# Three nine-column reciprocal roots: eleven VectorE operations each, or one GpSimd power each

## The chip, the core and the metric

One core of a Trainium2 chip runs the whole program in one launch. The metric is the device time of one execution in microseconds (us). Durations and starts come from one profiled execution; the engines are TensorE (PE in the rows, its weight loads PEld), VectorE (DVE), ScalarE (ACT), GpSimd (POOL) and SyncE (SP).

## The reference

One layer of a streaming encoder for 1024 new tokens (prompt) and 32 tokens of a running stream (sample), model width 1024. The input is normalised and projected; one half of the mixing width goes through a complex diagonal state-space scan with a gated linear unit, the other through latent attention with eight heads; each half is normalised, gated and projected back. Cut to what the change touches:

```python
def rmsnorm(x, g):
    xf = x.astype(jnp.float32)
    y = xf * lax.rsqrt(jnp.mean(xf * xf, axis=-1, keepdims=True) + EPS)
    return (y * g.astype(jnp.float32)).astype(x.dtype)

def mixer_layer(x, pos, h0, past_ckv, past_krope, p):
    h = rmsnorm(x, p['norm_in'])
    z = h @ p['w_in']
    u, g_ssm, c_q, c_kv, k_rope_raw, g_mla = jnp.split(z, cuts, axis=-1)
...
    mix = jnp.concatenate([rmsnorm(y_ssm, p['out_norm_ssm']) * jax.nn.silu(g_ssm),
                           rmsnorm(attn, p['out_norm_mla']) * jax.nn.silu(g_mla)], axis=-1)
    return x + mix @ p['w_out'], ckv, krope, h_last
```

The three norms here, of the token and of the two output halves, each need one reciprocal root per token: 1056 tokens, held as 128 partitions x 9 columns (eight columns of prompt tokens, one of sample tokens).

## The kernel before, in words

Products are done in two parts: each float32 operand is split into a rounded part and a rest (helpers `split`, `hilo`, lines 106 to 118: ScalarE rounds, VectorE subtracts), and three matmuls per product are accumulated in PSUM.

First stage (lines 206 to 304). The eight k slices of the transposed input are loaded and split. The input projection to the feature-major tiles (`mtile_mm`, line 231) takes 128 output features at a time: 8 k slices x 3 products x 3 column ranges of the 1056 tokens (384, 384, 288), 72 matmuls on line 235. Tiles 0 and 1 are accumulated while the input arrives and are copied raw to SBUF by ScalarE (line 298). The token norm is not applied to the input, but to the result: ScalarE squares the rows of x with a running sum (line 283), VectorE makes mean plus epsilon (line 284), `rsqrt` makes the root `rst` of nine columns (line 286), and `row_bcast` (line 178) turns it with nine TensorE transposes (line 185) and three ScalarE copies (line 187) into `rb`, a row of 1056 values on all partitions. `mtile_evac` (line 243) multiplies a tile with `rb` (lines 247, 251, 254). The four u tiles go through `uT`, which has two buffers, to DRAM (`u_out`, line 292) and are loaded back in another order (`load_u`). Tiles 2 and 3 are evacuated straight from PSUM, where six accumulators are set aside for these tiles, three a tile. Behind them on TensorE stand the preparations of the state-space matrices (`ssm_in`, lines 460 to 489) and the remaining eight tiles, the gates (line 720), which fill TensorE while VectorE does the scan.

Later stages: the scan (line 503), latent projections (`tok_mm`, line 572), the state-space outputs (line 677), the gated linear unit (line 705), expansion of queries and keys (lines 751 and 783, with roots of 12, 16 and 32 columns), then a half output projection (`half`, line 855) for the state-space half beside the start of the attention, the attention blocks (lines 970 to 1056), and the other half output projection at the end.

`col_rstd` (line 163) makes the root of an output half: nine matmuls with one output column sum the squares over partitions (line 170), VectorE adds epsilon (lines 172, 173), and `rsqrt` makes nine roots (line 175). For the state-space half it is `rsy` (line 728), used as a scale by ScalarE when it evacuates the products (`out_ssm`, line 885); for the attention half it is `rsa` (line 1174), called inside `half` at line 876 after the matmuls of the first two token tiles, and used by VectorE when it evacuates the products (`out_y`, line 1184). There GpSimd has added x and the other half's part before (line 1181).

`rsqrt` (line 151) is a first guess from the bits of the number (lines 155, 156) and three Newton steps of three operations (lines 158 to 160), eleven dependent VectorE operations; its two scratch buffers are a ring shared with the other roots.

What sets the order: the program is traced once, and a planner of the framework simulates it with its own costs and writes out each engine's queue: among instructions that are ready in that simulation the one that stands earlier in the program goes first. On the chip every engine works its queue strictly in that order. `issue_after` adds an edge that keeps an instruction behind another in a queue. GpSimd's queue holds, in program order, the constants at the start, the rotary tables (lines 736 to 739), the rotary products of the queries (lines 819 to 821), and, per attention block, the broadcast of the softmax sums (line 1042) and the squares, gates and splits of the output (lines 1070 to 1083), and at the end the sums of line 1181.

Of the kernel before, what the change touches and what calls it, by code (L numbers as in the profile page):

```python
# [16 lines left out]
ALU = mybir.AluOpType  # L17
# [18 lines left out]
TS = 9  # L36
# [14 lines left out]
def step(ctx: ExitStack, tc, xT, xr, winF, winT, wuq, wukv, wglu, wout, ckvcT, krcT, pk, rot, ssb, ssc, mtab,  # L51
         y_o, ckv_o, kr_o, st_o, dbg=None):
    nc = tc.nc
    pe, act, dve, pool, sp = nc.tensor, nc.scalar, nc.vector, nc.gpsimd, nc.sync
# [9 lines left out]
    def T(tag, shape, bufs=1, dt=F32, name=None):  # L64

        n = math.prod(shape[1:])
        t = sb.tile([128, -(-n // 264) * 264 if n > 400 else n], dt, tag=tag, name=name or tag, bufs=bufs)
        t = t[:shape[0], :n]
        if len(shape) == 3:
            t = t.rearrange("p (a b) -> p a b", a=shape[1])  # L70
        elif len(shape) == 4:
            t = t.rearrange("p (a b c) -> p a b c", a=shape[1], b=shape[2])
        return t

    marks = {}
# [10 lines left out]
    def PA(name="pa", tag="a"):  # L86
        return psA.tile([128, 512], F32, tag=tag, name=name, bufs=CAP[tag])
# [36 lines left out]
    def CC(n, p=128):  # L124
        taken[0] += n
        return base[:p, taken[0] - n:taken[0]]
# [12 lines left out]
    def SM(tag, shape, dt=F32, bufs=2):  # L139

        n = math.prod(shape)
        if tag not in ring:
            ring[tag] = [CC(n) for _ in range(bufs)]
        ring[tag].append(ring[tag].pop(0))
        t = ring[tag][-1].bitcast(dt)
        return t.rearrange("p (a b) -> p a b", a=shape[0]) if len(shape) == 2 else t

    onesD = CC(2)
    dve.memset(onesD[:, 0:1], 1.0 / D)
    dve.memset(onesD[:, 1:2], 1.0 / 512)  # L150
    def rsqrt(y, ms, n, p=128):

        t = SM("rq", [64])[:p, :n]
        s = SM("rqi", [64], I32)[:p, :n]
        dve.tensor_scalar(s, ms.bitcast(I32), 1, None, op0=ALU.logical_shift_right)
        dve.tensor_scalar(y.bitcast(I32), s, -1.0, float(0x5f3759df), op0=MUL, op1=ADD)
        for _ in range(3):
            dve.tensor_tensor(t, y, y, op=MUL)
            dve.scalar_tensor_tensor(t, ms, -0.5, t, op0=MUL, op1=MUL)
            r = dve.scalar_tensor_tensor(y, t, 1.5, y, op0=ADD, op1=MUL)  # L160
        return r.ins

    def col_rstd(ss, which, name):

        p = PA(name + "_p")
        ms = CC(TS)
        dve.memset(ms, 1.0)
        for i in range(TS):
            w = min(128, ss.shape[1] - i * 128)
            pe.matmul(p[:w, i:i + 1], ss[:, i * 128:i * 128 + w], onesD[:, which:which + 1],  # L170
                      start=True, stop=True)
        dve.tensor_scalar(ms[:, :TS - 1], p[:, :TS - 1], EPS, None, op0=ADD)
        dve.tensor_scalar(ms[:w, TS - 1:], p[:w, TS - 1:TS], EPS, None, op0=ADD)
        r = CC(TS)
        marks[name] = rsqrt(r, ms, TS)
        return r

    def row_bcast(r, dst):

        for c in range(3):  # L180
            p = PA("rb_p")
            n = 0
            for i in range(4 * c, min(TS, 4 * c + 4)):
                w = 128 if i < 8 else NS
                pe.transpose(p[:, n:n + w], r[:w, i:i + 1].to_broadcast([w, 128]), ident[:w, :w])
                n += w
            act.activation(dst[:, c * 512:c * 512 + n], p[:, :n], AF.Copy)
# [22 lines left out]
    for k in range(8):  # L210
# [8 lines left out]
        r = T("xr", [128, NT], 8)  # L219
# [55 lines left out]
    ssx = CC(TS)  # L275
# [7 lines left out]
        act.activation(t, t, AF.Square, accum_out=ssx[:, i:i + 1])  # L283
    dve.tensor_scalar(ssx, ssx, 1.0 / D, EPS, op0=MUL, op1=ADD)
    rst = CC(TS)
    marks["rst"] = rsqrt(rst, ssx, TS)
    row_bcast(rst, rb)
    for k in range(8):
        for j in range(2):
# [302 lines left out]
    def tok_group(gi, acc):  # L592
# [17 lines left out]
        dve.tensor_tensor(ss[:w, :n], ss[:w, :n], invn[:w, :n], op=MUL)  # L610
        dve.tensor_scalar(ss[:w, :n], ss[:w, :n], EPS, None, op0=ADD)
        rsqrt(rs[:w, :n].rearrange("p a b -> p (a b)"), ss[:w, :n].rearrange("p a b -> p (a b)"), 3 * n, w)
        kt = sm.tile([128, 4, 32], F32, tag="krt", name="krt")
        kr = sm.tile([128, 4, 32], F32, tag="kro", name="kro")
# [110 lines left out]
    for m in range(4):  # L725
        sp.dma_start(dgm[m], gate(8 + m, T("gm", [128, NT], 2), False))
    spread_s(ssy)
    rsy = col_rstd(ssy, 1, "rsy")
    mix = T("mix", [128, 4, NT])
    for m in range(4):  # L730
# [441 lines left out]
    def rsa():  # L1172
        spread_s(ssa)
        return col_rstd(ssa, 1, "rsa")
# [157 lines left out]
```

## Time and profile before

| what | us |
|---|---|
| median of three runs (583.57 to 587.38) | 585.41 |
| the profiled execution | 584.77 |
| its span, first to last instruction | 583.0 |
| TensorE busy (94%) | 547.1 |
| VectorE busy (71%), 1000 instructions | 414.8 |
| ScalarE busy (52%) | 304.4 |
| GpSimd busy (18%), 165 instructions | 107.5 |

Busy shares are means over stages with different limits. Times are from the start of the span. A timeline row gives start, duration, engine, line, operation, output and input by the program's names, shapes, how many were merged, and in brackets the engine's idle time before it and what ended that.

### The profile page before, as it was taken

The numbers are of one execution on the slowest core, as the hardware profiler recorded it, in microseconds if no ns is written. First come the engines' busy times: TensorE is split into PE (matmuls) and PEld (weight loads), VectorE is DVE, ScalarE is ACT, GpSimd is POOL, SyncE is SP. The second block draws the span as 40 slices with busy tenths as digits, with TensorE's granted clock in tenths as the row PEclk, the third lists the DMA queues.
The fourth block names the chain that finished last, engine by engine and source line by source line (L and its number), as shares of the span: only waits on it lengthen the run. The fifth ranks groups of instructions, "written<-read, shape, count | busy, mean of one in ns | idle before, by whom it ended". The sixth has DMA issues, their size and how long they took to land.

```text
span 583.0 us, 9939 instructions
## 1 busy us (share of the span) xinstructions
PE 547.1 (94%) x3707; PEld 481.5 (83%) x3707; DVE 414.8 (71%) x1000; ACT 304.4 (52%) x673; POOL 107.5 (18%) x165
## 2 busy tenths in 40 slices
PE   5989699999999997599999799999999999999997
PEld 5989599899999996599788578877778888877885
DVE  6999722989999254129989986668798577683722
ACT  5571155218135247639855966776676775752000
POOL 0000000000000010000024520222244334468330
PEclk9999799999999998889999899999999999999799
DMA  8991752232433204632401121200100101095352
GB/s 286 405 304 41 199 136 92 49 143 89 130 97 103 66 18 154 201 100 90 141 17 61 43 91 74 92 2 1 38 20 2 38 3 38 7 373 200 104 230 108
DMA packets 35266, 63.92 MB, mean 110 GB/s; under 512 B 5361, under 2 KB 21521, under 8 KB 35217
## 3 DMA queue, kind: packets, MB, share of 16 engines
q1 hardware_dynamic: 31008, 49.06, 25.9%
q10 hardware_dynamic: 4208, 14.22, 6.9%
q8 instruction: 29, 0.48, 0.3%
q14 instruction: 21, 0.16, 0.1%
HBM read 47.06 MB, written 16.21 MB: 109 GB/s over the span
## 4 chain that ended last, share of the span: by engine, by line
PE 74%; DVE 10%; ACT 5%; DMA 5%; issue 2%; POOL 2%; SPq 1%; ACTq 0%; DVEq 0%; POOLq 0%
PE mt L235 24%; PE wo L873 11%; PE ob L1048 6%; PE pt_p L1020 5%; PE S L980 3%; PE S L981 3%; PE S L982 3%; PE tk_p L585 2%; PE tk_p L584 2%; PE tk_p L586 2%; PE gl L705 2%; DMA yg<-dy 1%; PE ob L1049 1%; PE v_p L482 1%; PE qt_p L965 1%
## 5 line engine op out<-in xcount | busy, mean ns | idle before, releaser
L235 PE MATMUL mt<-xh,wh 128*128 128x384 f32 (+1 forms) x288 | 68.5, 335 | 11.9 <-ACT xh L112 6.2
L235 PE MATMUL mt<-xl,wh 128*128 128x384 f32 (+1 forms) x288 | 68.3, 331 | 0.1
L235 PE MATMUL mt<-xh,wl 128*128 128x384 f32 (+1 forms) x288 | 67.3, 330 | 0.0
L235 PEld LDWEIGHTS mt<-xh,wh 128*128 128x128 f32 x288 | 49.8, 193 | 13.5 <-ACT xh L112 6.8
L235 PEld LDWEIGHTS mt<-xl,wh 128*128 128x128 f32 x288 | 49.8, 193 | 1.0 <-issue 0.6
L235 PEld LDWEIGHTS mt<-xh,wl 128*128 128x128 f32 x288 | 49.2, 191 | 0.2 <-issue 0.2
L1020 PE MATMUL pt_p<-base,P 128*128 128x128 f32 x288 | 43.0, 276 | 0.8 <-ACT kv L769 0.7
L1048 PE MATMUL ob<-PT,kv 128*64 128x128 f32 x576 | 41.9, 279 | 0.9 <-DVE PT L1024 0.9
L873 PE MATMUL wo<-woh,mm 128*128 128x512 f32 x128 | 42.0, 398 | 0.3 <-DVE mm L110 0.3
L1048 PEld LDWEIGHTS ob<-PT,kv 128*64 128x64 f32 x576 | 32.0, 136 | 10.3 <-issue 7.2
L736 POOL TENSOR_TENSOR base<-base 128x288 f32<-128x288 f32 x1 | 0.9, 867 | 214.2 <-DVE kro L632 214.2
L1002 DVE TENSOR_REDUCE base<-S 128x1 f32<-128x1024 f32 (+3 forms) x32 | 32.4, 1017 | 10.3 <-PE S L982 10.2
L1004 ACT ACTIVATE P<-S,base 128x1024 f32<-128x1024 f32 (+3 forms) x32 | 30.6, 955 | 15.0 <-DVE base L1002 14.9
L1020 PEld LDWEIGHTS pt_p<-base,P 128*128 128x128 f32 x288 | 33.0, 140 | 5.1 <-ACT kv L769 1.0
L980 PE MATMUL S<-kTh,qTh 104*128 104x512 f32 (+3 forms) x96 | 36.2, 377 | 0.0
L1024 DVE COPY PT<-pt_p 128x512 f32<-128x512 f32 (+2 forms) x44 | 27.9, 635 | 9.3 <-PE pt_p L1020 9.1
L982 PE MATMUL S<-kTh,qTh 96*128 96x512 f32 (+3 forms) x96 | 34.2, 360 | 0.0
L981 PE MATMUL S<-kTl,qTh 96*128 96x512 f32 (+3 forms) x96 | 33.4, 348 | 0.0
L873 PEld LDWEIGHTS wo<-woh,mm 128*128 128x128 f32 x128 | 24.0, 189 | 6.2 <-DVE mm L110 0.7
L109 ACT ACTIVATE wh<-wr 128x512 fp32r<-128x512 f32 x24 | 14.1, 631 | 27.5 <-PE mt L235 25.9
L1184 DVE SCALAR_TENSOR_TENSOR yp<-wo,base,xt 128x512 f32<-128x512 f32 x16 | 11.6, 749 | 21.2 <-PE wo L873 21.2
L819 POOL TENSOR_TENSOR qx<-q,base 128x256 f32<-128x256 f32 (+1 forms) x12 | 8.3, 714 | 98.5 <-ACT q L801 83.0
(346 smaller groups left out, 1443.8 us busy)
## 6 DMA issues: line engine op xcount, KB each, us to landing
wr<-winF SPq DMA_DIRECT2D x10, 512.0 KB, 4.2
U<-du SPq DMA_DIRECT2D x8, 528.0 KB, 4.4
xr<-xr SPq DMA_DIRECT2D x8, 512.0 KB, 7.5
wor<-wout ACTq DMA_DIRECT2D x8, 512.0 KB, 4.3
dyp<-yp SPq DMA_DIRECT2D x8, 512.0 KB, 2.7
part<-dyp ACTq DMA_DIRECT2D x8, 512.0 KB, 5.3
xt<-xr ACTq DMA_DIRECT2D x8, 512.0 KB, 7.2
xr<-xT SPq DMA_DIRECT2D x7, 528.0 KB, 8.1
```

Source lines behind the costliest of these rows:

```text
L109: act.activation(hi, src, AF.Copy)
L235: pe.matmul(ps[c][:, :b - a], ww[:, k, :], xx[k][:, a:b], start=(k == 0 and first), stop=(k == 7 and last))
L584: pe.matmul(p, xhi[k][:, o:o + 128], h, start=(k == 0), stop=False)
L873: pe.matmul(s[i][c], mm[i][a][k], ww[k][b][:, c * 512:(c + 1) * 512], start=(k == 0 and first), stop=(k == 3 and last))
L980: pe.matmul(s[:, :n], qh[:, qj], kh[:, j, :n], start=True, stop=False)
L981: pe.matmul(s[:, :n], qh[:96, qj], kl[:, j, :n], start=False, stop=False)
L982: pe.matmul(s[:, :n], ql[:, qj], kh[:96, j, :n], start=False, stop=True)
L1002: dve.tensor_reduce(rl[:, 2 + j:3 + j], sf, AX.X, ALU.max, negate=True)
L1004: marks["exp", u] = act.activation(t[:, :n], sf, AF.Exp, bias=rl[:, 2 + j:3 + j], accum_out=rl[:, j:j + 1]).ins
L1020: pe.transpose(pp[:, (q - b) * 128:(q - b + 1) * 128], t[:, q * 128:(q + 1) * 128], ident)
L1024: dve.tensor_copy(ov, pp[:, :(e - b) * 128])
L1048: pe.matmul(ob[64 * j:64 * j + 64, r0:r0 + 128], v, t[:, b + q], start=(q == 0), stop=(q == nb - 1))
```

## The change

A column block of nine constants -0.5 is set once, a helper `rsqrt1` raises mean plus epsilon to that power with one GpSimd operation on 128 x 9 elements, and the three nine-column roots `rst`, `rsy` and `rsa` call it in place of `rsqrt`. The other roots (lines 612, 775, 806) stay as they are.

```diff
     onesD = CC(2)
     dve.memset(onesD[:, 0:1], 1.0 / D)
     dve.memset(onesD[:, 1:2], 1.0 / 512)
+    mhalf = CC(TS)
+    dve.memset(mhalf, -0.5)
+
+    def rsqrt1(y, ms):
+        return pool.tensor_tensor(y, ms, mhalf, op=ALU.pow).ins
+
     def rsqrt(y, ms, n, p=128):
...
         r = CC(TS)
-        marks[name] = rsqrt(r, ms, TS)
+        marks[name] = rsqrt1(r, ms)
         return r
...
     rst = CC(TS)
-    marks["rst"] = rsqrt(rst, ssx, TS)
+    marks["rst"] = rsqrt1(rst, ssx)
     row_bcast(rst, rb)
```

## Rows read from the trace of the kernel before

**Rows 1.** The page's chain that ended last, share of the span by engine.

```profile
PE 74%; DVE 10%; ACT 5%; DMA 5%; issue 2%; POOL 2%; SPq 1%; ACTq 0%; DVEq 0%; POOLq 0%
```

**Rows 2.** Busy by stretch: length, PE, PEld, DVE, ACT, POOL, PEclk, DMA, GB/s.

```profile
57.70:66.00 8.30, 3.43 (x37) 2.34 (x34) 7.23 (x16) 3.37 (x8) 0.00 (x0) 0.90 0.66 184
66.00:72.00 6.00, 5.90 (x21) 5.91 (x22) 3.52 (x9) 0.00 (x0) 0.00 (x0) 0.57 0.80 180
106.00:217.00 111.00, 111.00 (x700) 107.53 (x700) 89.96 (x211) 41.83 (x108) 1.08 (x2) 1.00 0.31 91
217.00:250.00 33.00, 22.24 (x153) 21.39 (x151) 12.24 (x15) 21.49 (x31) 0.71 (x2) 0.88 0.51 166
303.00:336.00 33.00, 29.55 (x127) 23.71 (x126) 32.46 (x81) 24.96 (x40) 17.14 (x18) 0.95 0.14 51
546.50:579.00 32.50, 32.50 (x141) 25.94 (x139) 11.29 (x16) 0.00 (x0) 4.81 (x2) 1.00 0.52 190
```

**Rows 3.** Timeline of TensorE, 57 to 67 us.

```profile
57.68 1.03 PE L185 MATMUL rb_p<-base 128*128 128x128 f32 x8
59.08 0.24 PE L185 MATMUL rb_p<-base 32*128 32x32 f32 x1 [0.36 <-ACT rb L187]
59.57 1.09 PE L460 MATMUL gt_p<-base,W 128*128 128x128 f32 x8 [0.25 <-ACT rb L187]
60.91 0.64 PE L466 MATMUL kpt<-W,ct 128*32 128x128 f32 x16 [0.25 <-ACT Gt L461]
62.06 0.44 PE L471 MATMUL kp<-base,kst 128*128 128x128 f32 x2 [0.51 <-ACT kst L469]
66.10 0.69 PE L235 MATMUL mt<-xh,wh 128*128 128x384 f32 x1 [3.60 <-DVE uT L251]
```

**Rows 4.** Timeline of VectorE, 45 to 66 us.

```profile
45.48 0.16 DVE L284 TENSOR_SCALAR base<-base 128x9 f32<-128x9 f32 x1
46.96 0.16 DVE L155 TENSOR_SCALAR base<-base 128x9 int32<-128x9 int32 x1
...
55.36 0.17 DVE L160 SCALAR_TENSOR_TENSOR base<-base 128x9 f32<-128x9 f32 x1
...
59.27 1.82 DVE L251 TENSOR_TENSOR uT<-ur,rb 128x384 f32<-128x384 f32 x4
...
65.48 1.35 DVE L251 TENSOR_TENSOR uT<-mt,rb 128x384 f32<-128x384 f32 x3 [0.71 <-DMA du<-uT]
```

**Rows 5.** Timeline of ScalarE, the copies of the broadcast root.

```profile
58.45 1.15 ACT L187 ACTIVATE rb<-rb_p 128x512 f32<-128x512 f32 x3
```

**Rows 6.** The chain of waits in order of time: start, duration, what.

```profile
61.23 4.24 DMA du<-uT
```

**Rows 7.** Groups of GpSimd by shape: busy us, mean ns, idle before them.

```profile
L1077 POOL TENSOR_TENSOR ats<-ats,base 128x32 f32<-128x32 f32 x4 | 1.0, 244 | 0.0
```

**Rows 8.** Timeline of VectorE and GpSimd, 539 to 547 us.

```profile
539.94 4.70 POOL L1181 TENSOR_TENSOR xt<-xt,part 128x1024 f32<-128x1024 f32 x2
540.46 1.88 DVE L155 TENSOR_SCALAR base<-base 128x9 int32<-128x9 int32 x1
...
546.93 3.38 DVE L1184 SCALAR_TENSOR_TENSOR yp<-wo,base,xt 128x512 f32<-128x512 f32 x5
```

**Rows 9.** Timelines of GpSimd, VectorE, ScalarE and TensorE, 215 to 330 us.

```profile
215.91 0.87 POOL L736 TENSOR_TENSOR base<-base 128x288 f32<-128x288 f32 x1 [214.20 <-DVE kro L632]
296.47 0.17 DVE L155 TENSOR_SCALAR base<-base 128x9 int32<-128x9 int32 x1
300.75 1.29 POOL L819 TENSOR_TENSOR qx<-q,base 128x256 f32<-128x256 f32 x2 [83.04 <-ACT q L801]
301.48 0.59 DVE L160 SCALAR_TENSOR_TENSOR base<-base 128x9 f32<-128x9 f32 x1
303.47 1.38 ACT L885 ACTIVATE yp<-wo,base 128x512 f32<-128x512 f32 x2 [0.52 <-PE wo L873]
329.93 0.50 PE L765 MATMUL kv_p<-uk,ckh 128*128 128x512 f32 x1 [3.19 <-ACT kv L769]
```

## The prediction

> **What bounds the kernel now.** I read the page's chain of waits first: three quarters of the chain that ends last are TensorE work [rows 1]. So an edit to short VectorE operations pays only where TensorE stands still for them. The table by stretch says where that is [rows 2]. From 106 to 217 us TensorE is busy 111.0 of 111.0 us, in the last stretch 32.5 of 32.5; but from 57.7 to 66.0 us only 3.43 of 8.30, and in the 6.0 us behind that it is busy at a granted clock of 0.57. From 217 to 250 us it is busy 22.24 of 33.0, for other reasons.
>
> TensorE's rows show the hole from inside [rows 3]: after the transposes of the token root at 57.68 come waits of 0.36, 0.25, 0.25, 0.51 and 3.60 us, 4.97 in all; at 66.10 it starts a tile whose accumulators had to be emptied by a multiplication with `rb`, the broadcast token root. VectorE's rows give the cause [rows 4]. The token mean is ready for the root at 45.48 + 0.16 = 45.64 us. The root is a dependent chain of eleven operations of 0.16 us, but they lie between other VectorE work: the first starts at 46.96, the last ends at 55.36 + 0.17 = 55.53, 9.9 us after its input. Then `rb` is copied out at 58.45 [rows 5], the first two u tiles are scaled from 59.27, the first is stored at 61.23 in 4.24 us [rows 6], and only at 65.48 does its buffer take the third u tile, whose accumulators TensorE waits for. So this root is on the path, although its own busy time is 11 x 0.16 = 1.8 us.
>
> **The change part by part.** Each of the three roots loses eleven VectorE operations and gets one GpSimd power. One memset of nine columns comes on top at the start, worth one operation of 0.16 us among work that waits for the first loads; I cost it at nothing, at most 0.2. The other roots stay on VectorE and keep their scratch ring, with three turns fewer.
>
> The power is in no row. From below: a GpSimd multiplication of 32 columns takes 0.244 us [rows 7]. From above, far off: one of 1024 columns with a sum takes 4.70 / 2 = 2.35 us [rows 8]. Nine columns lie by the first in shape, but a power is more work per element than a product; I take 1.0 us, four times the small row, and keep 0.24 to 2.35 as bounds. Beyond both rows a rival below asks what 10 us would do.
>
> *Token root.* GpSimd has nothing to do between its first 2 us and 215.91 us [rows 9], so the power starts when its input is there: 45.64 + 1.0 plus a short handover, some 47 us in place of 55.5. The order on each engine is made by the framework's planner, which takes the ready instruction that stands earliest in the program; `row_bcast` stands ahead of all the tiles that TensorE works on at 47 us. In the old order its transposes come after the whole of the third and fourth u tile, since the root was ready only then; I expect them some 9 us earlier, between matmuls of these tiles. ScalarE waits for nothing else then, so `rb` is out at about 50 us, the first u tile is scaled by 52, stored by 52 + 4.24 = 56.2, and the third takes its buffer by 57, before TensorE is through with its matmuls (57.68 + 1.2 for the transposes now ahead of them). So the wait of 3.60 goes. The other 1.37 us are short round trips to ScalarE for which matmuls can now be put in between; I take half, 0.7. The stretch behind ran at 0.57 because of the hole: 6.0 x 0.43 = 2.6 us were lost there, of which I take 2.4. Sum: 3.6 + 0.7 + 2.4 = 6.7 us. What is late next is TensorE itself, which is full to 217 us, so the shift carries through. Bounds: 0 if the planner moves nothing, 4.97 + 2.6 = 7.6 if all goes. With a power of 2.35 us `rb` is at 51.5, and all of this still holds.
>
> *Root of the SSM half.* Its chain runs from 296.47 to 301.48 + 0.6 us [rows 9] in a stretch where VectorE is busy 32.46 of 33.0 [rows 2] and TensorE waits once, 3.19 us at 329.93 for ScalarE. The power would give the root at 296.4 + 1.0, about 4 us sooner. The evacuation that uses it starts at 303.47, but TensorE has other matmuls up to 326, so the sooner root buys nothing by itself. VectorE gets some 2 us back (eleven steps of 0.1, two of them 0.5 longer under GpSimd's work), which may pull part of the wait at 329.93. On GpSimd the power stands between the rotary table, from 215.91, and the first rotary product at 300.75; it moves behind nothing and is done 3 us before that product. If the planner puts that group of products first, the root comes at about 305.5, 2.0 behind the evacuation's start. Bounds -2.0 to +2.0; I take 0.
>
> *Root of the attention half.* Its eleven operations run from 540.46 to 546.5, the first alone for 1.88 us beside GpSimd's two sums at 539.94, and the evacuations start at 546.93, behind one other operation [rows 8]. But TensorE works through the last stretch without a gap [rows 2], and the end hangs on it: a sooner root buys nothing. On GpSimd the power is ahead of these two sums (541.4 us), between them (543.4) or behind them (544.64 + 1.0 = 545.6): each is before 546.5, so nothing is lost. With 2.35 us and the last place it would be 547.0, 0.5 late. Queued behind the power are the sums for tiles 2 and 3, 1.5 us later at most; the first is wanted by the fifth evacuation, about 549 us. I take 0, bounds 0 to +1.
>
> Profiled execution 584.77 us, span 583.0 and 1.8 around it; it stands 0.6 below the median of the three runs, 585.41, within their spread. 584.77 - 6.7 = 578.1 us.
>
> **A rule of the Trainium skill against this.** In the trace GpSimd's first operation after 214.20 us of idling takes 0.87 us for 288 columns [rows 9], with no sign of a load of code. The Trainium skill (GPSIMD Engine Reference, section 2.1 Instruction dispatch) says that the first call of a freshly loaded GpSimd kernel pays about 6 us that no profile row shows; no run here shows it. By its figure, as an estimate, the token root would come near 53 us and the sum to about 584 us; by the row it stays at 578.1.
>
> **The rivals.** *Nothing gained.* The planner leaves the transposes behind both u tiles, or what is won before 217 us is given back between 217 and 250, where the path runs over transfers and ScalarE. For it: the order is rebuilt from 46 us on, and that stretch has 10.8 us of TensorE idle that can grow. Against: the program order favours the transposes, and scan, U loads and tiles all shift together. Time 583 to 587, say 585.
>
> *A late first power only.* Something delays the first power by 5 to 6 us and not the later ones. TensorE then stands at the transposes that the planner moved, up to 5 us, and the clock falls there in place of at 66 us; the two u tiles behind the transposes cover the old hole. Time 584.77 - 7 + 5 + 2 = 584 to 585. The skill's rule of the paragraph above would be this one.
>
> *Slower: the power is a long software routine*, about as long as the 9.9 us chain it replaces. In the token stage the transposes are in front of TensorE's queue at about 48.5 while the root comes at 56: 7.5 us lost, 5.0 of the old hole covered, +2.5. In the SSM half the root is 4 us later, up to +2. At the end it comes at 550 to 554 in place of 546.5; TensorE has accumulators for perhaps two more tiles and then waits, 4 to 8 us, and its clock falls after that, 2.4: +8. Sum 584.77 + 12 = 597. It decides from about 6 us a power (540.4 + 6 = 546.5). For it: no row shows a GpSimd function of this kind. Against: all GpSimd rows here are vector routines near 0.24 us plus 2 ns a column.
>
> *More gained.* All of 7.6 in the first stage, 2 us of VectorE's and 2 of the low clock behind 329.93: 584.77 - 11.6 = 573.
>
> *The change does not do what it says*: a power that leaves the eleven operations in is not possible by the diff, so no chance goes to it.
>
> **How the numbers follow.** Forecast case (575 to 582) 0.45; more gained 0.07; nothing gained 0.20; late first power 0.08; slow power 0.20. A measurement of this kernel can tell about 1% from no change, 5.9 us, so faster means under 579.5. Of the forecast case some three quarters lie below that, with the case of more gain 0.41; same: the rest of it, nothing gained, the late first power and a tenth of the slow case, 0.39; slower 0.20. The range that leaves out 2 in 10 reaches from the case of more gain to a power of about 8 us: 573 to 593. The forecast case's own is 575 to 582.
>
> **What would show it.** Right: a GpSimd power near 1 us at 46 to 47 us; TensorE's transposes at 47 to 50 between matmuls of u tiles three and four; no wait of 3.6 us near 66 and a clock near 1.0 in the 6 us behind it; the full stretch ending near 211 in place of 217; the last stretch without a gap. Wrong: a power above 6 us, TensorE waiting for GpSimd before its transposes or in the last 40 us, or an equal start of the tile at 66 us. If the stage gains and the total does not, the stretch from 217 to 250 has grown.

## The result, and the profile of the changed kernel

The change makes the kernel faster by about 1%: 578.58 us (576.58 to 580.78, six runs) beside 583.57 us for the kernel before on the same chip, ratio 0.990, 95% interval 0.9864 to 0.9936. A second comparison of the same pair gave 576.4 us beside 586.08, ratio 0.9853 (0.9822 to 0.9883). The forecast was 578.1. The profiled execution took 576.58 us, the fastest of its six, with a span of 574.8; it is read against the 583.0 of before, and this pair shows 8.2 us where the medians of the two comparisons show 5.0 and 9.7.

Lines behind 150 have numbers six higher than before (the tile's matmuls move from L235 to L241); the power is L155. The chain that ended last is TensorE's as before: 73% of the span, where [rows 1] has 74%.

Busy time by stretch; the columns are those of [rows 2]. The stretch from 212.70 is cut near the same work as the one from 217 there; the last one starts at the last sum of squares, where [rows 2] starts 6 us behind it:

```profile
57.70:66.00 8.30, 8.30 (x65) 7.93 (x65) 7.92 (x25) 2.40 (x5) 0.00 (x0) 1.00 0.85 219
66.00:72.00 6.00, 5.34 (x42) 5.02 (x40) 1.78 (x6) 2.33 (x13) 0.00 (x0) 1.00 1.17 256
106.00:212.70 106.70, 106.70 (x664) 103.55 (x662) 87.36 (x207) 39.35 (x105) 1.75 (x3) 1.00 0.30 91
212.70:243.00 30.30, 19.20 (x146) 18.37 (x145) 10.90 (x13) 21.46 (x31) 0.05 (x1) 0.94 0.54 181
532.60:570.40 37.80, 37.80 (x158) 30.43 (x158) 11.61 (x18) 0.00 (x0) 12.01 (x6) 0.95 0.45 166
```

The hole is filled: 8.30 of 8.30 us busy where [rows 2] has 3.43, and the 6 us behind it at full clock (2.4 GHz) where [rows 2] has 0.57. GpSimd's timeline shows the three powers, at 45.76, 288.08 and 533.26:

```profile
45.76 2.71 POOL L155 TENSOR_TENSOR base<-base 128x9 f32<-128x9 f32 x1 [44.04 <-DVE base L290]
...
288.08 1.80 POOL L155 TENSOR_TENSOR base<-base 128x9 f32<-128x9 f32 x1 [75.33 <-DVE base L162]
...
533.26 1.82 POOL L155 TENSOR_TENSOR base<-base 128x9 f32<-128x9 f32 x1
535.05 4.76 POOL L1187 TENSOR_TENSOR xt<-xt,part 128x1024 f32<-128x1024 f32 x2
```

The token power is 2.71 us long, yet the root is there at 48.5 in place of 55.5 [rows 4]. TensorE's timeline has its transposes at 51.17 in place of 57.68 [rows 3], between matmuls of the tiles:

```profile
51.17 1.03 PE L191 MATMUL rb_p<-base 128*128 128x128 f32 x8
51.96 0.55 PE L241 MATMUL mt<-xl,wh 128*128 128x384 f32 x2
...
55.50 0.24 PE L191 MATMUL rb_p<-base 32*128 32x32 f32 x1
...
287.23 0.28 PE L176 MATMUL rsy_p<-base,ssy 128*128 128x1 f32 x2
```

The ninth transpose, which in [rows 3] followed the eight at once, now stands 4.3 us behind them. The row at 287.23 is the last of the sums of squares of the SSM half. ScalarE's timeline: the copies of `rb` at 51.87 (58.45 in [rows 5]), and the first evacuation of the SSM half, 303.47 in [rows 9]:

```profile
51.87 1.09 ACT L193 ACTIVATE rb<-rb_p 128x512 f32<-128x512 f32 x2 [2.42 <-PE rb_p L191]
...
294.86 1.31 ACT L891 ACTIVATE yp<-wo,base 128x512 f32<-128x512 f32 x2 [0.57 <-PE wo L879]
```

VectorE's timeline: the token mean as the power's input, what runs beside the power, the first scaled u tiles and the third (65.48 in [rows 4]), and the evacuations of the last half (546.93 in [rows 8]):

```profile
45.51 0.17 DVE L290 TENSOR_SCALAR base<-base 128x9 f32<-128x9 f32 x1
45.59 1.21 DVE L446 TENSOR_TENSOR W<-W,ex 128x1024 f32<-128x1024 f32 x1
...
47.00 1.21 DVE L445 TENSOR_TENSOR ex<-bt,tmp 128x1024 f32<-128x1024 f32 x1
...
52.49 2.63 DVE L257 TENSOR_TENSOR uT<-ur,rb 128x384 f32<-128x384 f32 x6 [0.27 <-ACT rb L193]
...
58.83 1.34 DVE L257 TENSOR_TENSOR uT<-mt,rb 128x384 f32<-128x384 f32 x3
...
535.11 0.49 DVE L883 SCALAR_TENSOR_TENSOR base<-wos,base 128x256 f32<-128x256 f32 x1 [1.98 <-POOL base L155]
```

TensorE's table of waits has nothing left from 57.7 to 66 us. Its entry of 66 to 106 us is the first line below; the other two are those of 303 to 336 us:

```profile
PE gt_p L466 <- DVE ksb L482: 0.7, 1, 0.7
...
PE wo L879 <- DVE mm L110: 3.5, 1, 3.5
PE kv_p L771 <- ACT kv L775: 1.1, 2, 0.6
```

In the SSM half the old waits of 3.2 us for `kv` and 0.3 for `mm` have become 1.1 for `kv` and 3.5 for `mm`. The wait for `ksb` differs between executions: 0.7 us here, 2.2 in a second profile of the same kernel.

### The profile page after: what moved, and what is told of

It reads as the page before. It is cut to its first block, busy times and chain, and to the rows that moved or that the text cites. A ratio compares the mean times of both kernels' runs of the same rounds, so it can differ in the third digit from the quotient of the medians.

```text
span 574.8 us, 9915 instructions
## 1 busy us (share of the span) xinstructions
PE 542.8 (94%) x3707; PEld 476.7 (83%) x3707; DVE 407.6 (71%) x968; ACT 304.2 (53%) x673; POOL 114.1 (20%) x168
## 4 chain that ended last, share of the span: by engine, by line
PE 73%; DVE 11%; DMA 6%; ACT 4%; issue 3%; POOL 2%; SPq 1%; ACTq 0%; POOLq 0%; DVEq 0%
PE mt L241 22%; PE wo L879 11%; PE ob L1054 6%; PE pt_p L1026 6%; PE S L986 3%; PE S L988 3%; PE S L987 3%; DMA du<-uT 2%; PE tk_p L590 2%; PE tk_p L592 2%; PE tk_p L591 2%; PE gl L711 2%; DMA yg<-dy 1%; PE ob L1055 1%; PE qt_p L971 1%
## 5 line engine op out<-in xcount | busy, mean ns | idle before, releaser
L241 PE MATMUL mt<-xh,wh 128*128 128x384 f32 (+1 forms) x288 | 68.4, 333 | 7.9 <-ACT xh L112 5.8
L241 PE MATMUL mt<-xl,wh 128*128 128x384 f32 (+1 forms) x288 | 69.3, 332 | 0.1
L241 PE MATMUL mt<-xh,wl 128*128 128x384 f32 (+1 forms) x288 | 68.5, 330 | 0.0
L241 PEld LDWEIGHTS mt<-xh,wh 128*128 128x128 f32 x288 | 50.0, 193 | 9.2 <-ACT xh L112 6.3
L241 PEld LDWEIGHTS mt<-xl,wh 128*128 128x128 f32 x288 | 49.7, 193 | 1.0 <-issue 0.6
L241 PEld LDWEIGHTS mt<-xh,wl 128*128 128x128 f32 x288 | 49.5, 192 | 0.3 <-issue 0.2
L155 POOL TENSOR_TENSOR base<-base 128x9 f32<-128x9 f32 x3 | 6.3, 2110 | 119.4 <-DVE base L162 75.3
```

Source lines behind the costliest of these rows:

```text
L241: pe.matmul(ps[c][:, :b - a], ww[:, k, :], xx[k][:, a:b], start=(k == 0 and first), stop=(k == 7 and last))
```

## The experiments

What had to be settled: whether the gain is the token root's arrival, or VectorE's relief from 33 operations; whether the other two roots give or cost something; what a power costs and on what that depends; and what a late last root would cost.

**The token root alone, and the halves alone.** First the token power with the two halves on VectorE, then the reverse.

```diff
-        marks[name] = rsqrt1(r, ms)
+        marks[name] = rsqrt(r, ms, TS)
```

> Only the token root is a GpSimd power; the two output halves keep their eleven VectorE operations. Theory (arrival): the whole gain is TensorE's hole at 57.7 to 66 us, which closes because the token root arrives sooner. Then this kernel has nearly all of it: ratio 0.990 to 0.994, no TensorE wait above 1 us between 57.7 and 66 us, the last gate matmul near 213 us in place of 217.6. Rival (relief): the gain is spread over all three roots, since 33 operations leave a busy VectorE: ratio 0.995 to 0.998.

Measured: 576.22 us, ratio 0.9857 (0.9829 to 0.9886). The waits from 57.7 to 66 us are gone as in the full change; the next one is again for `ksb`, 1.4 us. The whole gain is here, and it is more than the 0.990 to 0.994 that was expected.

```diff
-    marks["rst"] = rsqrt1(rst, ssx)
+    marks["rst"] = rsqrt(rst, ssx, TS)
```

> Only the two output halves are GpSimd powers; the token root keeps its eleven VectorE operations. Theory (arrival): the wait of 3.6 us at 66 us stays, the last gate matmul stays near 217.6 us, the evacuations of the last stretch start some 3 us after the last sum of squares in place of 6.8, and the time does not change: ratio 0.997 to 1.001. Rival (relief): ratio 0.992 to 0.995.

Measured: 585.33 us beside 584.54, ratio 1.0034 (1.0005 to 1.0063): no gain, rather a small loss, just above the 0.997 to 1.001 that was expected. TensorE's waits from 57.7 to 106 us, and from 336 to 365:

```profile
PE mt L241 <- DVE uT L257: 3.9, 1, 3.9
...
PE wo L879 <- DVE mm L110: 3.5, 1, 3.5
```

The hole at 66 us stays, although VectorE has 22 operations fewer in all. Relief spread over all three roots falls as the cause; the arrival of the token root holds. Relief inside the token stage, where the power also takes eleven operations or 1.8 us from VectorE, is not tested apart by these two; the next run, which leaves them there, bears on it. The second line is the exchange of waits that the changed kernel shows in its SSM half.

**The state-space expansion held until the token root is done, roots on VectorE.** From the kernel before, to see whether the hole can be closed without GpSimd; to hold that order in SBUF, two buffers were given up.

```diff
-        with nullcontext():
+        with tc.issue_after(marks["rst"]) if m == 0 else nullcontext():
...
-        zz = [T("zt", [128, 2, 416], 3) for _ in range((n + 1) // 2)]
+        zz = [T("zt", [128, 2, 416], 2) for _ in range((n + 1) // 2)]
...
-        sq = T("sq", [128, NT], 2)
+        sq = T("sq", [128, NT], 1)
```

> All three roots stay on VectorE, no power. The state-space expansion of the first eight groups is held behind the token root in VectorE's queue, and two tiles (zt, sq) have one buffer less so that it fits; in TensorE's queue the transposes of the root stand 34 matmuls earlier than before (50 earlier with the power). Theory (arrival): what counts is when the root comes, not the engine: the root ends near 50 us in place of 55.5, the wait at 66 us is under 1 us, the last gate matmul is near 213 to 214 us, ratio 0.990 to 0.996 if the fewer buffers cost nothing. Rival (relief or engine): the wait at 66 us stays above 2 us, ratio 0.998 to 1.003.

Measured: 595.75 us, ratio 1.0177 (1.0142 to 1.0213). TensorE's waits from 57.7 to 66 us, then from 217 to 250:

```profile
PE mt L241 <- DVE uT L257: 1.7, 1, 1.7
...
PE cq_p L631 <- DVE zt L625: 8.8, 1, 8.8
```

With the expansion's operations out of the way the eleven steps lie closer: the root is done at 50.35 us on VectorE, where it was 55.53, and the wait of 3.60 shrinks to 1.7. That lies between the two expectations (under 1, above 2): it leans to arrival and does not settle it. The transposes run only at 53.71 here, and the held operations now stand between VectorE's scalings of the u tiles. The total missed, because something new stands at 217 us: a wait for the `zt` buffer that was taken away. So this total says nothing on roots on VectorE as such; one more run with that buffer missing, below, was needed for that.

**What a power costs.** Ahead of everything, on GpSimd: powers of 9, 9, 1, 16, 32 and 64 columns and a product of 9, their results unread.

```diff
+    for n in (9, 9, 1, 16, 32, 64):
+        pool.tensor_tensor(pout[:, :n], pin[:, :n], pex[:, :n], op=ALU.pow)
+    pool.tensor_tensor(pout[:, :9], pin[:, :9], pex[:, :9], op=MUL)
```

> The changed kernel with seven more GpSimd operations at the start, whose results nobody reads: powers of 9, 9, 1, 16, 32 and 64 columns and one product of 9. Theory (columns): a power costs a fixed part and a part per column; with 1.8 us for nine columns, about 0.4 for one, 3.0 for 16, 5.8 for 32, 11.4 for 64, and the first is as long as the second; the token root's power, 2.71 us in the changed kernel, is 1.8 plus 0.9 of waiting beside VectorE's 1.21 us addition and stays near 2.7. Rival (first call): the first power is some 0.9 us or more longer than the second, and the token root's falls to 1.8.

Measured: one run, 578.47 us. GpSimd's groups by shape (busy us, mean ns, idle before):

```profile
L159 POOL TENSOR_TENSOR pout<-pin,pex 128x64 f32<-128x64 f32 x1 | 11.1, 11126 | 0.1
...
L159 POOL TENSOR_TENSOR pout<-pin,pex 128x32 f32<-128x32 f32 x1 | 5.7, 5710 | 0.1
L159 POOL TENSOR_TENSOR pout<-pin,pex 128x9 f32<-128x9 f32 x2 | 3.6, 1807 | 0.1
L159 POOL TENSOR_TENSOR pout<-pin,pex 128x16 f32<-128x16 f32 x1 | 3.3, 3336 | 0.1
L159 POOL TENSOR_TENSOR pout<-pin,pex 128x1 f32<-128x1 f32 x1 | 0.7, 677 | 0.1
L160 POOL TENSOR_TENSOR pout<-pin,pex 128x9 f32<-128x9 f32 x1 | 0.3, 291 | 0.1
```

The first two powers in GpSimd's timeline:

```profile
1.86 1.81 POOL L159 TENSOR_TENSOR pout<-pin,pex 128x9 f32<-128x9 f32 x1
...
3.75 1.80 POOL L159 TENSOR_TENSOR pout<-pin,pex 128x9 f32<-128x9 f32 x1
```

A power grows with its columns, (11.126 - 5.710) / 32 = 0.169 us each; a product of nine columns takes 0.29 us, a power of nine 1.81. The first of the two nine-column powers took 1.81 and the second 1.80 us, and the second starts 0.08 us behind the end of the first, so there is no cost of a first one. The token power, now the seventh on the engine, is as long as in the changed kernel, in GpSimd's timeline:

```profile
45.70 2.70 POOL L163 TENSOR_TENSOR base<-base 128x9 f32<-128x9 f32 x1 [18.61 <-DVE base L298]
```

So its extra 0.9 us belong to its place. From 45.59 to 46.80 VectorE runs a two-input addition of 1024 columns beside it.

**The full change and its parts in one comparison.** The changed kernel, the token root alone, and the token root with either half, all beside the same runs of the kernel before (586.08 us). The third has

```diff
-        marks[name] = rsqrt1(r, ms)
+        marks[name] = rsqrt1(r, ms) if name == "rsy" else rsqrt(r, ms, TS)
```

and the fourth the same with "rsa".

> The changed kernel itself, on one chip with the three that follow. Theory (only the token root pays, the output halves cost a little): ratio to the kernel before 0.988 to 0.992, and the token root alone (next run) 0.2% to 0.5% below it. Rival (no difference): both within 0.2% of each other.

> The token root alone as a power, again, beside the changed kernel on the same chip. Theory: ratio 0.984 to 0.989, that is 1 to 3 us below the changed kernel. Rival (no difference): the same ratio as the changed kernel within 0.2%.

> Token root and root of the SSM half as powers, the attention half on VectorE. If the SSM half's power is what costs (GpSimd's 1.8 us, during which VectorE is full), this is like the changed kernel, ratio 0.988 to 0.992; if it costs nothing, like the token root alone, 0.984 to 0.988.

> Token root and root of the attention half as powers, the SSM half on VectorE. If the attention half's power costs nothing, since TensorE works through the last stretch without a gap, this is like the token root alone, 0.984 to 0.988; the evacuations of the last stretch start 3 us after the last sum of squares in place of 6.8 with no gain. If it costs, 0.988 to 0.992.

| kernel | us | ratio, 95% interval |
|---|---|---|
| the full change | 576.4 | 0.9853 (0.9822 to 0.9883) |
| token root alone | 576.2 | 0.9849 (0.9816 to 0.9882) |
| token and SSM half | 579.39 | 0.9887 (0.9852 to 0.9921) |
| token and attention half | 577.74 | 0.9865 (0.9832 to 0.9898) |

After the first two runs I held that the halves cost a little on top of the token root. That theory is not borne out: the full change and the token root alone are 0.2 us apart. The third run lies in the range that was named for a cost, but the intervals of all four overlap; a cost or gain of the halves below some 2 us can't be told by these runs.

**One power more ahead of the token root.** From the changed kernel; its result is overwritten by the real one. One `zt` buffer was given up as above.

```diff
+    pool.tensor_tensor(rst, ssx, mhalf, op=ALU.pow)
     marks["rst"] = rsqrt1(rst, ssx)
```

> The changed kernel with a second power of the token mean into the same nine columns, so that the root comes 1.8 us later, and the tile zt with one buffer less so that it fits. In TensorE's queue the transposes stand 12 matmuls later than in the changed kernel, 38 earlier than before. Theory (arrival, with some slack): no TensorE wait above 1 us between 57.7 and 72 us still, since the hole was 5 us and the root still comes 5 us sooner than before. On the total: if the slower time of the run that held the expansion (1.018) came from the missing buffers of zt and sq, this one is slow too, ratio above 1.00, with a TensorE wait of some 9 us for zt behind 217 us; if it came from the roots on VectorE, this one is at 0.985 to 0.992.

Measured: 587.47 us, ratio 1.0051 (1.0028 to 1.0074). GpSimd's timeline, the transposes in TensorE's, then TensorE's waits from 57.7 to 66 us and from 217 to 250:

```profile
46.05 2.71 POOL L292 TENSOR_TENSOR base<-base 128x9 f32<-128x9 f32 x1 [44.33 <-DVE base L290]
48.84 2.59 POOL L155 TENSOR_TENSOR base<-base 128x9 f32<-128x9 f32 x1
```

```profile
51.90 1.04 PE L191 MATMUL rb_p<-base 128*128 128x128 f32 x8
```

```profile
PE mt L241 <- DVE uT L257: 0.2, 1, 0.2
...
PE cq_p L632 <- DVE zt L626: 8.8, 1, 8.8
```

With the root 3.0 us later, at 51.43 in place of 48.47, the transposes run only 0.73 us later than in the changed kernel, and the old wait is back by 0.2 us only (and one of 0.4 for `kpt`). The stage has room for about one power more: in the changed kernel the transposes stand 2.70 us behind the root, at their place in TensorE's queue. The root is also later here than in the run that held the expansion (50.35), and yet the wait is shorter than its 1.7. So the finish of the root alone does not set the wait; the order that the planner makes from it, on TensorE and on VectorE, does its part. The total again carries the 8.8 us for the `zt` buffer, now with all roots on GpSimd, and a granted clock of 0.54 from 222 to 228 us, behind that wait. So at least that much of the slow total of the held expansion came from the buffer, not from the roots. The rest, 595.75 - 587.47 = 8.3 us, is open.

**A late last root.** Here the sums of the residual on GpSimd, all but the first, are held behind the last split of the attention's output; first in the changed kernel, then in the kernel before.

```diff
-        pool.tensor_tensor(x, x, part, op=ADD)
+        with tc.issue_after(marks["fin"]) if i else nullcontext():
+            pool.tensor_tensor(x, x, part, op=ADD)
```

> The changed kernel with GpSimd's sums of line 1187 (x plus the other half's part), all but the first, held behind the attention's last split in GpSimd's queue. In the changed kernel one of them takes 3.4 us at 523.8 in the middle of the last block's squares, gates and splits, and the chain that ends last runs through it. Theory: the last sum of squares and the last matmuls start about 3.4 us sooner, ratio to the kernel before 0.978 to 0.984, that is 2 to 4 us under the changed kernel. Rival: the sums are late for the evacuations, TensorE waits for accumulators in the last 30 us, ratio 0.985 or more.

Measured: 577.22 us, ratio 0.9887 (0.9856 to 0.9917), no better than the change: the theory missed, and the time lies in the rival's range. The power did not come sooner: the planner put two sums ahead of it. GpSimd's timeline, then TensorE's from the first matmul behind the sums of squares to the one that waits:

```profile
534.34 4.76 POOL L1188 TENSOR_TENSOR xt<-xt,part 128x1024 f32<-128x1024 f32 x2
539.07 1.82 POOL L155 TENSOR_TENSOR base<-base 128x9 f32<-128x9 f32 x1
```

```profile
533.86 0.48 PE L879 MATMUL wo<-woh,ath 128*128 128x512 f32 x1
...
539.30 0.39 PE L879 MATMUL wo<-woh,atl 128*128 128x512 f32 x1
541.56 0.48 PE L879 MATMUL wo<-woh,ath 128*128 128x512 f32 x1 [1.87 <-DVE base L883]
```

> The kernel before with the same hold of the sums. Theory: the end gains the same 2 to 4 us without any power, ratio 0.993 to 0.997, and the wait at 66 us stays. Rival: no gain, since VectorE's eleven operations of the last root then stand beside six sums in a row and are late: 0.998 or more.

Measured: 590.7 us, ratio 1.0103 (1.0068 to 1.0138), slower, as the rival said. VectorE's timeline, with the second step of the root and the factors behind the last, and the same view of TensorE:

```profile
543.05 2.26 DVE L162 TENSOR_SCALAR base<-base 128x9 int32<-128x9 int32 x1
...
553.51 0.49 DVE L883 SCALAR_TENSOR_TENSOR base<-wos,base 128x256 f32<-128x256 f32 x1
```

```profile
542.40 0.48 PE L879 MATMUL wo<-woh,ath 128*128 128x512 f32 x1
...
547.83 0.39 PE L879 MATMUL wo<-woh,atl 128*128 128x512 f32 x1
554.15 0.77 PE L879 MATMUL wo<-woh,ath 128*128 128x512 f32 x1 [5.93 <-DVE base L883]
```

Both kernels give one number: after the last sum of squares TensorE has work for 5.8 us, 24 matmuls (533.86 to 539.69 and 542.40 to 548.22, at a granted clock of 1.00), and then stands until the factors are there: 1.9 us in the one, 5.9 in the other. This is the price that the slower rival named.

## Why the prediction was right, point by point

**The number.** 578.58 us stands 0.5 from the forecast of 578.1, and that closeness is in part luck: the forecast took 6.7 us off 584.77, the measurement took 5.0 off 583.57, and the second comparison shows 9.7.

**Token root.** The mechanism came as forecast: the power started at 45.76 and was done at 48.5 (said some 47), transposes between matmuls at 51.17 (said 47 to 50), third u tile at 58.83 (said 57), no wait of 3.6 us, and a clock of 1.00. Each event is 1 to 2 us later than said, and one term was mis-sized: the power. I took 1.0 us between 0.24 and 2.35; alone it takes 1.80, and here 2.71, above my upper bound. The bound came from an addition's row, and per column a power is far dearer than that. It cost nothing, and it does not explain the later events: the transposes start 2.70 us behind the power's end and without a wait, and a root 3.0 us later still moved them by 0.73. Their place in TensorE's queue sets them.

**The sum of the stage.** I said 6.7 us. The waits of 4.97 that lay between 57.7 and 66.1 us are gone entirely, not to 4.3; one of 0.7 is new behind them; and the low clock's part is back, 5.90 us of busy time from 66 to 72 us at 0.57 [rows 2], some 2.5. That makes 4.97 - 0.7 + 2.5 = 6.8 us, where I said 6.7 and at most 7.6. The full stretch was to end near 211 in place of 217; the `ck_p` matmul ahead of its last gate matmuls starts at 212.62 in place of 217.57, a shift of only 4.95. No other work stands ahead of it, but the profiled execution of the changed kernel had half the clock for a while before any power ran. TensorE's stretches (columns of [rows 2]) in the kernel before, at that place, up to `ck_p` and behind it:

```profile
34.50:38.00 3.50, 3.50 (x22) 3.50 (x23) 3.47 (x15) 3.50 (x8) 0.00 (x0) 1.00 1.07 348
0.00:217.50 217.50, 204.13 (x1321) 196.19 (x1322) 162.22 (x463) 90.48 (x224) 2.74 (x10) 0.98 0.46 145
217.60:583.00 365.40, 342.87 (x2388) 285.16 (x2386) 252.47 (x538) 213.95 (x449) 104.65 (x156) 0.97 0.26 89
```

and in the changed kernel:

```profile
34.50:38.00 3.50, 3.50 (x13) 3.50 (x14) 3.46 (x15) 3.50 (x8) 0.00 (x0) 0.51 1.07 337
0.00:212.55 212.55, 203.83 (x1321) 195.88 (x1322) 161.50 (x453) 89.95 (x224) 5.46 (x11) 0.99 0.47 148
212.60:574.80 362.20, 338.93 (x2388) 280.81 (x2386) 246.00 (x516) 214.21 (x449) 108.60 (x158) 0.98 0.26 90
```

The same 1321 matmuls are ahead of `ck_p` in both. From 34.5 to 38 us the changed kernel did 13 in place of 22 of them, 3.50 x 0.49 = 1.7 us lost, and 4.95 + 1.7 = 6.7 is nearly the sum above. In the second profile of the same kernel that stretch is at full clock, but the wait for `ksb` is 2.2 us, and `ck_p` starts at 212.68; the sum is 5.3 there.

Behind `ck_p` this pair gains 3.2 us more, which no step of the prediction names. From 217 to 250 nothing was given back: from that `ck_p` to the first matmul of the gated linear unit it is 29.5 us (242.1), where it was 30.8 (248.4). Up to the end the same 2388 matmuls are busy 3.9 us less, at a clock of 0.98 in place of 0.97, and the waits are no shorter (23.3 us, were 22.5). So the part behind is clock, and where the clock falls differs between executions. In the profile of the token root with the attention half the wait for `ksb` is 2.4 us, the clock from 72 to 81 us is 0.62, and `ck_p` starts at 217.74, as late as before; its span of 576.6 us is still 6.4 shorter than 583.0. The closed hole is shown, and the stage's sum by its waits and its clock; how much of one execution's total comes from it, and whether the change makes low clock rarer behind it, is open.

**SSM half, said 0.** The runs with and without it can't be told apart. The reason given is shown too: between the last matmuls of the sums of squares and the first evacuation lie 303.47 - 295.89 = 7.58 us before and 294.86 - 287.23 = 7.63 after, though the root takes one power of 1.80 in place of eleven steps. TensorE's output matmuls set that start. What I hoped for at best, a part of the wait at 329.93, didn't come. I had read one wait there, and there were two: 3.2 us for `kv` and 0.3 for `mm`. They are now 1.1 and 3.5, no shorter in sum.

**Attention half, said 0.** The power ran ahead of the two residual sums, and the evacuations start 535.51 - 532.8 = 2.7 us behind the last sum of squares where it was 6.8. It bought nothing, as said. But my reason was thinner than I put it. I read a last stretch without a gap from 546.5 us on [rows 2]. The 6.3 us ahead of it, in the kernel before, look like this:

```profile
540.20:546.50 6.30, 6.30 (x17) 4.97 (x18) 5.92 (x13) 0.00 (x0) 4.44 (x2) 0.57 0.00 0
```

They have no gap either, but 17 matmuls at a granted clock of 0.57. So the 24 matmuls behind the sums of squares lasted from 540.02 to 548.37, 8.3 us, and the factors, ready at 546.53 + 0.48 = 547.0, were 1.4 us ahead of their end. At full clock they last 5.8 us, by the two held runs, and would have ended some 1.2 us before the factors, as an estimate. With the token root alone that stretch has a clock of 0.75, and the root on VectorE is already a little late, as TensorE's wait says:

```profile
PE wo L879 <- DVE base L883: 0.2, 1, 0.2
```

So the zero is right, but it hung on a low clock and not on a surplus of accumulators. No run has this root on VectorE at full clock with the sums in their old place.

**The rivals.** A late first power: no, 1.81 and 1.80 us for the first two, with 0.08 us between them, and in the changed kernel the transposes that read the first power ran 2.70 us behind its end. The Trainium skill (GPSIMD Engine Reference, section 2.1 Instruction dispatch), by whose 6 us for the first call of a freshly loaded kernel the time would have been about 584, is not borne out for this operation. The slow power: no, at 1.8 us; its mechanism is real, and a power of 32 columns, 5.7 us, with the 0.4 us ahead of it and the 0.5 behind it in the changed kernel, would outlast the 5.8 us of accumulators, as an estimate. Nothing gained: no; it is what the halves alone give. More gained: the stage gave 6.8 of the 7.6 us that this case counted there, and the halves nothing that these runs can tell. By the prediction's own shares "same" adds up to 0.41 and "slower" to 0.18, not to 0.39 and 0.20.

## What to carry to other kernels

A chain of short operations is to be priced by when its result arrives, not by its busy time: 1.8 us of VectorE work took 9.9 us to arrive, and a slower engine with an empty queue gave it in 2.7. Move only the chain that a full engine waits for; the other two roots, moved in the same way, gave nothing. Before such a change is spread to wider tiles, look at the price per column, 0.169 us here, and before a buffer is given up for another order, look at who waits for it: one `zt` buffer was worth 8.8 us of TensorE.

## What the runs showed of the hardware

A power of two tensors on GpSimd is far dearer than a product of the same shape: 1.81 us against 0.29 for nine columns, 5.71 against the 0.244 of [rows 7] for 32. Beside VectorE's two-input addition the same power took 2.71 us, and the addition kept its 1.21. The reverse shows at the end of the kernel: a one-input VectorE operation of nine columns takes 2.26 us beside GpSimd's sums, and 0.17 without them. The Trainium skill (SBUF — State Buffer, Who interferes with whom) has one pair of ports that VectorE and GpSimd share under an exclusive lock. The first delay agrees with that: the addition still had 46.80 - 45.76 = 1.04 us to go when the power started, and the power is 0.91 longer. A lock for the whole of the power is not what the rows show: a second two-input addition ran inside it, from 47.00 us, and took the same 1.21 us as the first. For the second delay no row shows which ports the nine-column operation used.
